# The recurrent branch's output projection as seven products of halves, with the pool branch's output tiles ahead

## The chip, the cores and the metric

The kernel runs on one core of a Trainium2 chip. The metric is the device time of one execution in microseconds. The core's engines work side by side, each through its own list of instructions in order: TensorE (PE in the profile, with its weight loads as PEld) multiplies matrices into eight PSUM banks, VectorE (DVE), ScalarE (ACT) and GpSimd (POOL) do the elementwise work, and SyncE (SP) issues DMA transfers. POOL issues some too. An instruction starts when its engine has reached it and its operands are ready.

## The reference

One block of a hybrid decoder, for 512 tokens of width 1024, in float32. In short:

```
h    = rms_norm(x, g_mix_pre)
u_pool, xb, gb, gates = split(h @ w_in)          # 512, 1024, 1024, 2 x 1024 wide
y_pool = pool_mixer(u_pool) @ w_pool_out         # 512 -> 1024
y_rnn  = rg_lru_branch(xb, gb) @ w_rg_out        # 1024 -> 1024
m    = sigmoid(gate_0) * y_pool + sigmoid(gate_1) * y_rnn
x    = x + rms_norm(m @ w_o, g_mix_post)
x    = x + rms_norm(gated ConvFFN(rms_norm(x)))  # w_up (1024 -> 2 x 3072), w_down
x    = x + rms_norm(gated input embedding p)     # out
```

The change concerns the third and fourth of these lines, `y_rnn` above all: a product of a 512×1024 matrix (tokens × channels) with the 1024×1024 weight `w_rg_out`. The kernel keeps activations with channels on the 128 partitions and tokens along the free dimension.

## The kernel before

**Products.** A float32 product is made of three TensorE products: each operand is split into a high part (rounded to the type fp32r) and a low part (the rest), and `mm3` multiplies high by high, high by low and low by high (lines 220 to 222 of the profile). A split is a copy on ScalarE (`hi`) and a subtraction on VectorE (`lo`, line 190). Weights come as 512 KB tiles (128×1024) by SP into `raw`, and are split into `hi` and `lo`; each of the three has six buffers. The function `weight` asks for a weight and has the next four of a fixed list (`order`) loaded and split too.

**Seven products.** A product of two matrices that are cut into 2×2 blocks can be made of seven products of half blocks, with sums and differences of blocks on either side (Strassen's form). The kernel has this for `w_o`, `w_up` and `w_down`: the sums of weight blocks (numbers 4 to 7; 1 to 3 are plain blocks) are made in DRAM by DMAs that add, issued by POOL at the start (`sum_in_dram`: first 16 for `w_o`, then 16 for `w_up`; those of `w_down` come later). The activations' sums ("forms") are made by VectorE and then split. The two output projections `w_pool_out` and `w_rg_out` are plain before.

**Early blocks.** Ten weight blocks (products 3, 7 and 4 of `w_o`, two each, and four of `w_up`) are loaded, split and written back to DRAM as `parts`, high and low, ahead of time (`split_early`), and later loaded as `hi` and `lo` straight away. Each is one load and two writes of 512 KB on SP's queue.

**Order.** TensorE's list is in the order of the code. The other engines' lists are set by a scheduler by priorities that follow the code's order; `urgent` raises those of evacuations. SP's list holds all loads and the `parts` writes, in one order, so that a write whose source isn't ready holds up the loads behind it. The names in the order below: `raw`, `hi`, `lo` are weight tiles, `ps` a PSUM bank, `m`, `t`, `C`, `A` are activation tiles, `parts` and the `sum` tiles lie in DRAM. A number behind a name tells buffers apart.

**The stages around the change.** The loop over `IN_ORDER` makes the gates' 16 tiles (`gate_step`), with the pooling and its maps between them; from its step `EARLY_AT` = 20 on it splits one early block a step. At gate tiles 5 and 8 the recurrent branch's output is split (`rnn_split`). Then a loop over the eight output tiles m: four `mm3` for `w_pool_out` (12 matmuls of 512 columns), eight for `w_rg_out` (24), then three VectorE operations (gate times each bank, and their sum into `mq`, lines 879 to 881), and one more early block in each turn (six in all). Behind it comes `w_o` by seven products in the order `SERIAL` = 1, 2, 5, 6, 3, 7, 4, whose forms are made by `o_form` out of `mq`.

Of the kernel before, what the change touches and what calls it, by code (L numbers as in the profile page):

```python
# [14 lines left out]
P = 128  # L15
# [67 lines left out]
def block_kernel(  # L83
# [161 lines left out]
    def rows2(w, kp, h):  # L245
# [22 lines left out]
    def up_block(p, f):  # L268

        j = (f % 10 - 1) * NJ + 2 * p  # L270
        h = f // 10 - 1
        return w_up[j : j + 2, :, h * S : (h + 1) * S].rearrange("j p c -> p j c")

    usum = {(p, f): dram.tile([P, 2, S], F32, name=f"up{p}sum{f}") for p in UP_SUMS for f in (5, 6, 7, 4)}

    def sums_of(name):

        if name == "up":
            for p in UP_SUMS:
                for f, start, more in ((5, 11, 12), (7, 12, 22), (6, 5, 22), (4, 6, 21)):  # L280
                    yield usum[p, f], usum[p, start] if start < 10 else up_block(p, start), {}
                    yield usum[p, f], up_block(p, more), {"accum_op": ALU.add}
# [122 lines left out]
    def prep(key):  # L405
        if key[0] == "up" and key not in parts:
            up_form(*key[1:])
            return
        if key in parts:
            hi, lo = parts_of(D)  # L410
            for i, v in enumerate((hi, lo)):
                nc.sync.dma_start(v.bitcast(F32), parts[key][i])
            if key[0] == "up":
                hi, lo = (v.rearrange("p (j c) -> p j c", j=2) for v in (hi, lo))
            ready[key] = (hi, lo)
            return
        ap = src[key]
        n = 1
        for d in ap.shape[1:]:
            n *= d  # L420
        raw = wpool.tile([P, n], F32, tag="raw", name=nm("raw"), bufs=6)
        dst = raw if len(ap.shape) == 2 else raw.rearrange("p (k c) -> p k c", k=ap.shape[1])
        if key == order[0]:
            nc.sync.dma_start(xraw[0], x_t[0])
            for a, b in FIRST:
                nc.sync.dma_start(raw[:, a:b], ap.rearrange("p k c -> p (k c)")[:, a:b])
        else:
            nc.sync.dma_start(dst, ap)
        hi, lo = parts_of(n)
        if key == order[0]:  # L430
            for a, b in FIRST:
                ACT.copy(hi[:, a:b], raw[:, a:b])
                sub(lo[:, a:b], raw[:, a:b], hi[:, a:b].bitcast(F32))
        else:
            ins = ACT.copy(hi, raw)  # L435
            if key[0] == "wpg" and key[2] == 1:
                behind(ins, last_copy[0].ins.name)
            with tc.high_priority(offset=2 * URGENT if key[0] == "wpg" and key[2] == 0 else 300 if key[0] == "in" and key[1] >= 12 else 0):
                ins = sub(lo, raw, hi.bitcast(F32))
                low_of[key] = ins.ins.name  # L440
            if key[0] == "wpg" and key[2] == 1:
                behind(ins, last_low[0])
        ready[key] = (hi, lo)

    def weight(key, ahead=AHEAD):
# [235 lines left out]
    yh = [None, None]  # L681
    yl = [None, None]

    def rnn_out(cs):
        for c in cs:
            act(rg_t[c], rg_t[c], AF.Gelu_apprx_tanh)
            V.tensor_tensor(r_t[c], r_t[c], rg_t[c], ALU.mult)
# [32 lines left out]
    rnn_out(range(8))  # L720


    yp, pools = {}, {}

    def pool_tile(g):
        w = WINDOWS[g]
# [21 lines left out]
    def pool_map(g):  # L748
        pw = weight("pool_w")
        ps = bank()  # L750
        mm3(ps, pick(pw, g * P, (g + 1) * P), pools[g], True, True)
        hi, lo = slot(F32R), slot(F32R)
# [7 lines left out]
    def gate_tile(m):  # L760
        ps = in_tile(16 + m)
        g = slot()
        with tc.high_priority(offset=300):
            scaled(ps, g)
        act(g, g, AF.Sigmoid)
        gate[m] = g
        if m in SPLIT_AT:
            rnn_split(SPLIT_AT.index(m))

    for n, step in enumerate(IN_ORDER):  # L770
        split_early(1 if n >= EARLY_AT else 0)
# [64 lines left out]

    def o_form(f):

        h11, h12, h21, h22 = (halves(mq[k], b) for b in range(2) for k in range(2))
# [20 lines left out]
        return v[:, 0], v[:, 1]  # L860


    mq = [quad("A", F32), quad("A", F32)]
    for m in range(KD):
        w = weight(("wpo", m))
        pa = bank()
        for k in range(4):
            mm3(pa, pick(w, k * P, (k + 1) * P), yp[k], k == 0, k == 3)
        w = weight(("wrg", m))
        if m == KD - 1:  # L870
            o_form(1)
# [10 lines left out]
        if m == KD - 1:  # L882
            o_form(2)
        if m == PLE_AT:
            pled = dram.tile([S, D], F32, name="pled")
            pq = []
            for k in range(2):
# [60 lines left out]

        return tuple(v[c][b] for v in (h2h, h2l))

    def products(o, w, i, form, start):
        for k in range(4):
            lhs = tuple(v[:, i, k * P : (k + 1) * P] for v in w)
            rhs = tuple(v[:, k, :] for v in form)
            mm3(o, lhs, rhs, start and k == 0, k == 3, near, skip_group_check=True)

    def up_plain(f, b):
        for i in range(2):
            d = gb if f % 10 == 1 else ub
# [21 lines left out]
                V.scalar_tensor_tensor(h2n[t, h], res[h], r, g_pre[h], ALU.mult, ALU.mult)  # L981


    oz, o11, o12, od5 = ([bank(), bank()] for _ in range(4))
# [420 lines left out]
```

## Time and profile before

| | us |
|---|---|
| median of three runs | 704.36 (704.07 to 704.71) |
| profiled execution, its own time | 703.83 |
| its span, first to last instruction | 702.1 |
| TensorE busy | 696.5 |
| VectorE busy | 574.1 |
| ScalarE busy | 440.9 |
| GpSimd busy | 82.9 |
| pool output and recurrent output tiles on TensorE | 202.6 to 264.8 |

The busy time of an engine is that of the whole span; a stage can be limited by something else than the mean shows. A row of the windows gives the busy time of each engine in a stretch of the span, with the number of instructions in parentheses. A row of the timeline gives the start, the duration, the engine, the source line, the operation, output and input, and in brackets the engine's idle time before it and what ended that. A row of the DMA view gives a queue's packets, its megabytes and the share of the 16 DMA engines' time that they took.

### The profile page before, as it was taken

The numbers are of one execution on the slowest core, as the hardware profiler recorded it, in microseconds if no ns is written. First come the engines' busy times: TensorE is split into PE (matmuls) and PEld (weight loads), VectorE is DVE, ScalarE is ACT, GpSimd is POOL, SyncE is SP. The second block draws the span as 40 slices with busy tenths as digits, with TensorE's granted clock in tenths as the row PEclk, the third lists the DMA queues.
The fourth block names the chain that finished last, engine by engine and source line by source line (L and its number), as shares of the span: only waits on it lengthen the run. The fifth ranks groups of instructions, "written<-read, shape, count | busy, mean of one in ns | idle before, by whom it ended". The sixth has DMA issues, their size and how long they took to land.

```text
span 702.1 us, 11239 instructions
## 1 busy us (share of the span) xinstructions
PE 696.5 (99%) x4279; PEld 637.0 (91%) x4279; DVE 574.1 (82%) x749; ACT 440.9 (63%) x670; POOL 82.9 (12%) x107
## 2 busy tenths in 40 slices
PE   9999999999999999999999999999999999999997
PEld 8888888888888888899999999999999888888886
DVE  5698645999656568777989999997999999788972
ACT  6857789953543245468866667765767766665631
POOL 0221111110000000121013232121300000001100
PEclk9999999999999999999999999999999999999999
DMA  8999986656698999996479999998976577868111
GB/s 320 406 314 244 227 229 153 157 165 219 237 327 285 323 334 374 332 317 218 152 286 240 278 297 266 304 239 299 241 200 233 203 250 235 283 206 273 47 61 60
DMA packets 65077, 172.54 MB, mean 246 GB/s; under 512 B 5952, under 2 KB 6592, under 8 KB 64704
## 3 DMA queue, kind: packets, MB, share of 16 engines
q1 hardware_dynamic: 50480, 129.88, 53.2%
q0 software_dynamic: 14400, 41.95, 25.5%
q8 instruction: 33, 0.54, 0.3%
q14 instruction: 20, 0.16, 0.1%
q10 hardware_dynamic: 144, 0.00, 0.0%
HBM read 155.03 MB, written 58.72 MB: 304 GB/s over the span
## 4 chain that ended last, share of the span: by engine, by line
PE 99%; DVE 0%; ACT 0%; issue 0%
PE ps L220 31%; PE ps L222 31%; PE ps L221 31%; PE ps L541 3%; PE ps L913 1%; PE ps L650 1%; PE ps L239 1%; PE ps L592 0%; ACT t L165 0%; DVE t L1323 0%; DVE t L1324 0%; PE ps L1034 0%; DVE m L231 0%; DVE mhalf L233 0%
## 5 line engine op out<-in xcount | busy, mean ns | idle before, releaser
L190 DVE TENSOR_TENSOR lo<-raw,hi 128x1024 fp32r<-128x1024 f32 (+2 forms) x193 | 224.0, 1184 | 60.2 <-ACT hi L435 42.3
L220 PE MATMUL ps<-A,hi 128*128 128x256 f32 (+1 forms) x608 | 194.4, 320 | 0.0
L221 PE MATMUL ps<-A,hi 128*128 128x256 f32 (+1 forms) x608 | 193.8, 319 | 0.0
L222 PE MATMUL ps<-A,lo 128*128 128x256 f32 (+1 forms) x608 | 193.8, 319 | 0.0
L435 ACT CAST hi<-raw 128x1024 fp32r<-128x1024 f32 (+1 forms) x112 | 112.0, 1011 | 80.6 <-PE ps L222 27.6
L220 PEld LDWEIGHTS ps<-A,hi 128*128 128x128 f32 x608 | 115.9, 191 | 8.2 <-issue 1.0
L222 PEld LDWEIGHTS ps<-A,lo 128*128 128x128 f32 x608 | 116.0, 191 | 6.8
L221 PEld LDWEIGHTS ps<-A,hi 128*128 128x128 f32 x608 | 116.0, 191 | 6.8
L220 PE MATMUL ps<-C,hi 128*128 128x256 f32 (+1 forms) x392 | 114.5, 292 | 0.0
L222 PE MATMUL ps<-C,lo 128*128 128x256 f32 (+1 forms) x392 | 114.3, 292 | 0.0
L221 PE MATMUL ps<-C,hi 128*128 128x256 f32 (+1 forms) x392 | 114.3, 292 | 0.0
L194 ACT CAST hi<-raw 128x1024 fp32r<-128x1024 f32 x78 | 80.3, 1050 | 24.5 <-PE ps L221 14.5
L220 PE MATMUL ps<-hi,A 128*128 128x512 f32 x224 | 85.2, 380 | 0.0
L221 PE MATMUL ps<-lo,A 128*128 128x512 f32 x224 | 84.9, 379 | 0.0
L222 PE MATMUL ps<-hi,A 128*128 128x512 f32 x224 | 84.9, 379 | 0.0
L220 PEld LDWEIGHTS ps<-C,hi 128*128 128x128 f32 x392 | 74.7, 191 | 1.9
L221 PEld LDWEIGHTS ps<-C,hi 128*128 128x128 f32 x392 | 74.7, 191 | 1.8
L222 PEld LDWEIGHTS ps<-C,lo 128*128 128x128 f32 x392 | 74.7, 191 | 1.7
L462 POOL TENSOR_TENSOR s<-s,mhalf 128x1 f32<-128x1 f32 (+1 forms) x21 | 16.2, 773 | 336.9 <-DVE s L478 315.1
L220 PEld LDWEIGHTS ps<-hi,A 128*128 128x128 f32 x224 | 42.3, 189 | 6.3 <-ACT hi L435 0.3
L222 PEld LDWEIGHTS ps<-hi,A 128*128 128x128 f32 x224 | 42.3, 189 | 6.0
L221 PEld LDWEIGHTS ps<-lo,A 128*128 128x128 f32 x224 | 42.3, 189 | 5.8
(191 smaller groups left out, 1024.0 us busy)
## 6 DMA issues: line engine op xcount, KB each, us to landing
raw<-in_w_up_dram SPq DMA_DIRECT2D x46, 512.0 KB, 7.7
wdsum<-in_w_down_dram POOLq DMA_DIRECT2D x36, 512.0 KB, 9.2
raw<-in_w_in_dram SPq DMA_DIRECT2D x32, 512.0 KB, 6.9
raw<-wdsum SPq DMA_DIRECT2D x24, 512.0 KB, 4.5
raw<-in_w_down_dram SPq DMA_DIRECT2D x18, 512.0 KB, 4.0
wosum<-in_w_o_dram POOLq DMA_DIRECT2D x12, 512.0 KB, 9.0
wdsum<-wdsum POOLq DMA_DIRECT2D x12, 512.0 KB, 6.9
parts<-hi SPq DMA_DIRECT2D x10, 512.0 KB, 5.0
```

The costliest lines, as they stand in the source:

```text
L190: return V.tensor_tensor(o, a, b, ALU.subtract)
L194: last_copy[0] = ACT.copy(hi, src)
L220: PE.matmul(o, ah, bh, start=start, stop=False, **kw)
L221: PE.matmul(o, ah, bl, start=False, stop=False, **kw)
L222: PE.matmul(o, al, bh, start=False, stop=stop, **kw)
L239: PE.matmul(wps[:, :P], ones, ones, start=True, stop=True)
L435: ins = ACT.copy(hi, raw)
L462: last_pow[0] = nc.gpsimd.tensor_tensor(y, v, mhalf[:, :n], ALU.pow).ins.name
L541: PE.matmul(rx[m], a[:, o : o + P], turns(b), start=k == 0 and i == 0, stop=k == KD - 1 and i == 2)
L650: PE.matmul(ps, bd[pr, a, o], turns(b[pr]), start=i == 0, stop=i == 2)
L913: PE.transpose(ps[:, q * P : (q + 1) * P], a[:, q * P : (q + 1) * P], ident)
```

## The change

The eight `w_pool_out` tiles are all made first, each into a bank of its own, and multiplied by the gate at once (line 918 of the changed kernel). Then `w_rg_out` is made by seven products in the order `RSEVEN` = 1, 5, 6, 2, 3, 7, 4, in two groups of four output tiles: 2 groups × 7 products × 2 tiles × 4 steps × 3 matmuls = 336 of 256 columns, where 192 of 512 stood. The recurrent output's forms are made in place: form 1 at gate tile 5, form 4 at 8, the differences at 9 to 11, and the forms 5, 6, 3 and 7 in the loop over the pool tiles, form 2 behind it. Partial sums of several products lie in shared banks, copied from one to another by ScalarE and merged with the gates by VectorE in `merge` (lines 931 to 934, 256 columns each, 20 operations a group). Eight sums of weight blocks are new, each made by two DMAs on POOL's queue, ahead of those of `w_o` and `w_up`. The early blocks start at step 16 in place of 20: eight are made in the gates' loop and two at the pool tiles 5 and 6. The copy of `p` into its form moves behind the first group.

```diff
-EARLY_AT = 20
-SPLIT_AT = 5, 8
+EARLY_AT = 16
+FORMS_AT, RSUMS_AT = {5: 1, 8: 4}, (9, 10, 11)
...
+RSEVEN = (1, 5, 6, 2, 3, 7, 4)
...
-PLE_AT = 3
+LATE_FORMS = {0: 5, 1: 6, 2: 3, 4: 7}
...
-        name: w.rearrange("(q a s p) c -> q s p a c", a=2, s=2, p=P) for name, w in (("wo", w_o), ("wd", w_down))
+        "wo": w_o.rearrange("(s q a p) c -> q s p a c", s=2, a=2, p=P),
+        "wd": w_down.rearrange("(q a s p) c -> q s p a c", a=2, s=2, p=P),
...
+    def rg_block(p, f):
+
+        j, h = 4 * p + 2 * (f % 10 - 1), f // 10 - 1
+        return w_rg_out[j : j + 2, :, h * S : (h + 1) * S].rearrange("j p c -> p j c")
+
+    rsum = {(p, f): dram.tile([P, 2, S], F32, name=f"rg{p}sum{f}") for p in range(2) for f in (5, 6, 7, 4)}
...
     for m in range(KD):
         plan(("wpo", m), w_pool_out[m])
-        plan(("wrg", m), w_rg_out[m])
+    for p in range(2):
+        for f in RSEVEN:
+            plan(("rg", p, f), rsum[p, f] if (p, f) in rsum else rg_block(p, {1: 11, 2: 21, 3: 22}[f]))
...
-    sum_in_dram(chain_of(sums_of("wo"), sums_of("up")), None)
+    sum_in_dram(chain_of(sums_of("rg"), sums_of("wo"), sums_of("up")), None)
...
-    def rnn_split(i):
-        yh[i], yl[i] = quad("C"), quad("C")
+    rform = {}
+
+    def rg_half(k, b):
+        return [r_t[4 * k + q][:, b * HALF : (b + 1) * HALF] for q in range(4)]
+
+    def rg_sum(o, a, b, op=ALU.subtract):
         for q in range(4):
-            split(yh[i][:, q, :], yl[i][:, q, :], r_t[4 * i + q])
+            V.tensor_tensor(o[q], a[q], b[q], op)
+
+    def rg_form(f):
+
+        h = [[rg_half(k, b) for b in range(2)] for k in range(2)]
+        if f == 3:
+            rg_sum(h[0][0], h[0][0], h[1][0], ALU.add)
+        v = {1: h[0][0], 2: h[1][0], 4: h[1][1], 5: h[1][1], 6: h[0][0], 3: h[0][0], 7: h[0][1]}[f]
+        w = quad("C" if f in (1, 2, 4) else "A").rearrange("p (s a) (b c) -> p s (a b) c", s=2, b=2)
+        for q in range(4):
+            split(w[:, 0, q, :], w[:, 1, q, :], v[q])
+        rform[f] = w[:, 0], w[:, 1]
...
-    mq = [quad("A", F32), quad("A", F32)]
+    mq, pas = [], []
     for m in range(KD):
         w = weight(("wpo", m))
-        pa = bank()
+        if m in LATE_FORMS:
+            rg_form(LATE_FORMS[m])
+        if m >= 5:
+            split_early(1)
+        pas.append(bank())
         for k in range(4):
-            mm3(pa, pick(w, k * P, (k + 1) * P), yp[k], k == 0, k == 3)
-        w = weight(("wrg", m))
-        if m == KD - 1:
-            o_form(1)
-        split_early(1)
-        pb = bank()
-        for k in range(KD):
-            y = yh[k // 4][:, k % 4, :], yl[k // 4][:, k % 4, :]
-            mm3(pb, pick(w, k * P, (k + 1) * P), y, k == 0, k == KD - 1)
-        a, b = gate[m], gate[8 + m]
+            mm3(pas[m], pick(w, k * P, (k + 1) * P), yp[k], k == 0, k == 3)
         with urgent():
-            V.tensor_tensor(row(a), back(pa), row(a), ALU.mult)
-            V.tensor_tensor(row(b), back(pb), row(b), ALU.mult)
-            V.tensor_tensor(mq[m % 2][:, m // 2, :], a, b, ALU.add)
+            V.tensor_tensor(row(gate[m]), back(pas[m]), row(gate[m]), ALU.mult)
+    rg_form(2)
+
+    rz, rd, rq = [bank(), bank()], bank(), {}
+    ra, rb2 = pas[4:6], pas[6:8]
+
+    def merge(p, n, i, b):
+
+        m, hs = 4 * p + 2 * n + i, slice(b * HALF, (b + 1) * HALF)
+        g, v = gate[8 + m][:, hs], (ra, rb2)[n][i][:, hs]
+        with urgent():
+            if n:
+                t = temp()[:, :HALF]
+                V.tensor_tensor(t, v, rq[p][:, i * HALF : (i + 1) * HALF], ALU.add)
+                v = t
+            V.tensor_tensor(row(g), back(v), row(g), ALU.mult)
+            V.tensor_tensor(mq[p][:, 2 * n + i, hs], gate[m][:, hs], g, ALU.add)
+
+    def rg_product(p, f):
+        for i in range(2):
+            w = weight(("rg", p, f))
+            o = {1: rz, 6: rz, 7: rz, 2: ra, 4: ra, 3: rb2, 5: (rd, rd)}[f][i]
+            a = HALF if f == 4 or (f, i) == (5, 1) else 0
+            products(o[:, a : a + HALF], w, i, rform[f], f in (1, 5), turns)
+            z = rz[i][:, :HALF]
+            with urgent():
+                if f == 1:
+                    ACT.copy(ra[i][:, :HALF], z)
+                elif (f, i) == (5, 1):
+                    rq[p] = temp()
+                    ACT.copy(rq[p], rd)
+                elif f == 6:
+                    ACT.activation(rb2[i][:, :HALF], z, AF.Identity, scale=-1.0)
+                elif f == 7:
+                    ACT.copy(ra[i][:, HALF:], z)
+                    ACT.activation(rb2[i][:, HALF:], z, AF.Identity, scale=-1.0)
+            if f in (2, 3, 7, 4):
+                merge(p, int(f in (3, 7)), i, int(f in (7, 4)))
+
+    for p in range(2):
+        for f in RSEVEN:
+            if f == 2:
+                mq.append(quad("C", F32))
+            rg_product(p, f)
+            if (p, f) == (1, 6):
+                o_form(1)
+            if (p, f) == (1, 3):
+                o_form(2)
+        if p == 0:
```

How the lists of three engines stand is shown at the places that the prediction speaks of. POOL's list, from the end of the first norm on, where the sums of weight blocks are issued; before:

```order
L295 DMA wosum_104<-in_w_o_dram 256x1x512 x4
L295 DMA wosum_106<-in_w_o_dram 256x1x512 x4
L295 DMA wosum_105<-wosum_104 16x8192 x2
L295 DMA wosum_105<-in_w_o_dram 256x1x512 x2
L295 DMA wosum_107<-wosum_105 16x8192 x2
L295 DMA wosum_107<-in_w_o_dram 256x1x512 x2
L295 DMA up1sum_112<-in_w_up_dram 256x1x512 x2
```

and changed:

```order
L304 DMA rg0sum_112<-in_w_rg_out_dram 256x1x512 x2
L304 DMA rg0sum_114<-in_w_rg_out_dram 256x1x512 x2
L304 DMA rg0sum_113<-rg0sum_112 16x8192
L304 DMA rg0sum_113<-in_w_rg_out_dram 256x1x512
L304 DMA rg0sum_115<-rg0sum_113 16x8192
L304 DMA rg0sum_115<-in_w_rg_out_dram 256x1x512
L304 DMA rg1sum_116<-in_w_rg_out_dram 256x1x512 x2
L304 DMA rg1sum_118<-in_w_rg_out_dram 256x1x512 x2
```

Sixteen DMAs for the recurrent weight stand first, and those of `w_o` and `w_up` follow in their old order.

SP's list at the end of the gates' loop, from the load of the last weight of that loop on; before:

```order
L428 DMA raw308_1728<-in_w_in_dram 128x1024
L355 DMA raw313_1762<-in_w_o_dram 128x2x512
L428 DMA raw316_1770<-in_w_pool_out_dram 128x512
L355 DMA raw321_1804<-in_w_o_dram 128x2x512
L889 DMA t391_2177<-in_p_t_dram 128x512
L889 DMA t394_2183<-in_p_t_dram 128x512
L428 DMA raw324_1812<-in_w_rg_out_dram 128x1024
L355 DMA raw329_1846<-wosum7_106 128x1024
L428 DMA raw332_1854<-in_w_pool_out_dram 128x512
L359 DMA parts3_120<-hi314_1764 128x1024
L359 DMA parts3_120<-lo315_1765 128x1024
```

and changed, from the row behind the same load on:

```order
L370 DMA parts3_128<-hi294_1704 128x1024
L370 DMA parts3_128<-lo295_1705 128x1024
L366 DMA raw317_1822<-wosum4_107 128x1024
L370 DMA parts4_129<-hi298_1718 128x1024
L370 DMA parts4_129<-lo299_1719 128x1024
L370 DMA parts5_130<-hi306_1764 128x1024
L370 DMA parts5_130<-lo307_1765 128x1024
L370 DMA parts6_131<-hi310_1778 128x1024
L370 DMA parts6_131<-lo311_1779 128x1024
L370 DMA parts7_132<-hi318_1824 128x1024
L370 DMA parts7_132<-lo319_1825 128x1024
L439 DMA raw320_1830<-in_w_pool_out_dram 128x512
```

The first pool-output weight stood ahead of all `parts` writes and stands behind ten of them now.

VectorE's list at the end of the stage, where `w_o`'s forms are made (`C467` and `C483` are the form of product 5, `A474` and the like its and other forms' low parts); before:

```order
L880 TENSOR_TENSOR m344_1927<-ps435_2392,m344_1927 128x512
L881 TENSOR_TENSOR A346_1931<-m275_1575,m344_1927 128x512
L190 TENSOR_TENSOR lo463_2485<-raw461_2482,hi462_2484 128x1024
L190 TENSOR_TENSOR A436_2420<-A346_1931,A436_2420 128x1024
L845 TENSOR_TENSOR C467_2513<-A345_1930,A346_1931 128x1024
```

and changed, the last rows up to the same form:

```order
L931 TENSOR_TENSOR t453_2689<-ps390_2192,t434_2538 128x256
L933 TENSOR_TENSOR m324_1861<-ps372_2116,m324_1861 128x256
L933 TENSOR_TENSOR m348_1987<-t453_2689,m348_1987 128x256
L934 TENSOR_TENSOR C439_2575<-m225_1343,m324_1861 128x256
L934 TENSOR_TENSOR C439_2575<-m274_1598,m348_1987 128x256
L933 TENSOR_TENSOR m332_1903<-ps379_2144,m332_1903 128x256
L191 TENSOR_TENSOR lo476_2760<-raw474_2757,hi475_2759 128x1024
L934 TENSOR_TENSOR C439_2575<-m240_1423,m332_1903 128x256
L191 TENSOR_TENSOR lo479_2785<-raw477_2782,hi478_2784 128x1024
L883 TENSOR_TENSOR C483_2813<-C405_2314,C439_2575 128x1024
```

Merges of 256 columns, up to three for one piece of an output tile, stand where two or three of 512 columns closed one tile.

More of the change, by code (lines that the diff above doesn't have):

```diff
@@ L272, in up_block @@
         return w_up[j : j + 2, :, h * S : (h + 1) * S].rearrange("j p c -> p j c")
+    def rg_block(p, f):
+        j, h = 4 * p + 2 * (f % 10 - 1), f // 10 - 1
+        return w_rg_out[j : j + 2, :, h * S : (h + 1) * S].rearrange("j p c -> p j c")
+    rsum = {(p, f): dram.tile([P, 2, S], F32, name=f"rg{p}sum{f}") for p in range(2) for f in (5, 6, 7, 4)}
     usum = {(p, f): dram.tile([P, 2, S], F32, name=f"up{p}sum{f}") for p in UP_SUMS for f in (5, 6, 7, 4)}
     def sums_of(name):
-        if name == "up":
-            for p in UP_SUMS:
+        if name in ("up", "rg"):
+            sums, of, ps = (usum, up_block, UP_SUMS) if name == "up" else (rsum, rg_block, range(2))
+            for p in ps:
                 for f, start, more in ((5, 11, 12), (7, 12, 22), (6, 5, 22), (4, 6, 21)):
-                    yield usum[p, f], usum[p, start] if start < 10 else up_block(p, start), {}
-                    yield usum[p, f], up_block(p, more), {"accum_op": ALU.add}
+                    yield sums[p, f], sums[p, start] if start < 10 else of(p, start), {}
+                    yield sums[p, f], of(p, more), {"accum_op": ALU.add}
             return
@@ L442, in prep @@
                 behind(ins, last_low[0])
+        if key[0] == "rg":
+            hi, lo = (v.rearrange("p (j c) -> p j c", j=2) for v in (hi, lo))
         ready[key] = (hi, lo)
@@ L837, in o_form @@
     def o_form(f):
-        h11, h12, h21, h22 = (halves(mq[k], b) for b in range(2) for k in range(2))
+        h11, h12, h21, h22 = (halves(mq[k], b) if k < len(mq) else None for b in range(2) for k in range(2))
         v = {1: h11, 2: h12, 4: h22}.get(f)
@@ L860, in o_lhs, with products @@
         return v[:, 0], v[:, 1]
[L863 removed]
+    def products(o, w, i, form, start, order=near):
+        for k in range(4):
+            lhs = tuple(v[:, i, k * P : (k + 1) * P] for v in w)
+            rhs = tuple(v[:, k, :] for v in form)
+            mm3(o, lhs, rhs, start and k == 0, k == 3, order, skip_group_check=True)
+    mq, pas = [], []
     for m in range(KD):
         w = weight(("wpo", m))
[L866 to L884 removed]
+        if m in LATE_FORMS:
[3 more added lines that the diff above has]
+        pas.append(bank())
+        for k in range(4):
+            mm3(pas[m], pick(w, k * P, (k + 1) * P), yp[k], k == 0, k == 3)
+        with urgent():
+            V.tensor_tensor(row(gate[m]), back(pas[m]), row(gate[m]), ALU.mult)
@@ L949, in h2 @@
         return tuple(v[c][b] for v in (h2h, h2l))
[L951 to L955, printed above, removed]
     def up_plain(f, b):
@@ L981, in x2_out @@
                 V.scalar_tensor_tensor(h2n[t, h], res[h], r, g_pre[h], ALU.mult, ALU.mult)
-    oz, o11, o12, od5 = ([bank(), bank()] for _ in range(4))
+    o11, o12 = ra, rb2
+    oz, od5 = ([bank(), bank()] for _ in range(2))
     o5 = wpool.tile([P, 2, S], F32, tag="sum", name=nm("sum"), bufs=1)
```

22 lines of the change are left out of this document (16 added, 6 removed).

## Prediction

> **What bounds the kernel now.** I read the engine shares and the chain first. The first row of the chain is TensorE alone, and no matmul group of the page has idle time before it: what is taken off TensorE shortens the run, and any wait put into TensorE lengthens it by its own length.
>
> ```profile
> span 702.1 us, 11239 instructions
> PE 696.5 (99%) x4279; PEld 637.0 (91%) x4279; DVE 574.1 (82%) x749; ACT 440.9 (63%) x670; POOL 82.9 (12%) x107
> PE 99%; DVE 0%; ACT 0%; issue 0%
> L221 PE MATMUL ps<-A,hi 128*128 128x256 f32 (+1 forms) x608 | 193.8, 319 | 0.0
> ```
>
> The second view is the table of windows, cut where the stages change: the gate tiles end at 202.6, the two output projections run to 264.8, then `w_o` begins. After each time range stand PE, PEld, DVE, ACT and POOL busy with their counts, the granted clock, the busy share of the 16 DMA engines, and GB/s.
>
> ```profile
> 162.00:182.00 20.00, 20.00 (x95) 17.44 (x94) 19.57 (x33) 10.71 (x16) 0.00 (x0) 1.00 0.49 172
> 182.00:202.60 20.60, 20.60 (x97) 18.05 (x96) 12.29 (x14) 8.99 (x12) 0.00 (x0) 1.00 0.94 338
> 202.60:264.80 62.20, 62.20 (x289) 54.45 (x289) 39.92 (x49) 23.59 (x29) 0.00 (x0) 1.00 0.90 313
> 264.80:301.00 36.20, 36.20 (x173) 31.73 (x172) 29.12 (x35) 18.04 (x30) 3.00 (x3) 1.00 0.96 350
> 400.00:500.00 100.00, 100.00 (x898) 100.00 (x897) 92.30 (x100) 63.84 (x106) 25.38 (x32) 1.00 0.99 279
> ```
>
> TensorE has no gap in any of them. But in the stage that changes, the DMA engines are 0.90 busy already and DVE has 22 us free. The third view shares each window between the two DMA queues: q1 carries SP's transfers, q0 the weight sums that POOL issues (packets, MB, share of the 16 engines). The rows are of 28–52 us (two queues at work), 202.6–264.8 and 264.8–301 (SP's alone).
>
> ```profile
> q1 hardware_dynamic: 1447, 5.27, 55.0%
> q0 software_dynamic: 1109, 2.96, 47.9%
> ```
> ```profile
> q1 hardware_dynamic: 7430, 19.40, 89.5%
> ```
> ```profile
> q1 hardware_dynamic: 4283, 12.64, 96.2%
> ```
>
> So SP's queue alone moved 12.64 MB in 36.2 us (349 GB/s), in the changed stage 312, and 219.6 GB/s while sums took half of the engines. "DMA: Bandwidth & Descriptors" of the Trainium skill, section "Queues, rings and completion order", says that each engine takes the queues with work in turn, a packet at a time; the 55.0% and 47.9% agree.
>
> **The change, TensorE's part.** The recurrent projection's 8×8×3 = 192 matmuls of 512 columns become 2×7×2×4×3 = 336 of 256. The stage 202.6–264.8 holds 288 wide ones: 62.2/288 = 0.216 us each. For narrow ones, at full clock:
>
> ```profile
> 419.73 0.28 PE L220 MATMUL ps<-C,hi 128*128 128x256 f32 x1
> ...
> 424.87 0.28 PE L221 MATMUL ps<-A,hi 128*128 128x256 f32 x1
> ```
>
> 46 steps in 5.14 us are 0.1117 each. 192×0.216 = 41.5; 336×0.1117 = 37.5: **−4.0 us**, all on the path. Moving the eight pool-output tiles forward changes no count. A smaller piece with a sign of its own: product 7 is followed at once by product 4, which accumulates on ScalarE's copy of 7; I price that at 0 (other bounds: 0 to 2×0.6).
>
> **VectorE's part.** Durations are pitches of back-to-back work: two 1024-wide ones take 2.25 us from 141.81 to 144.06 (1.125 each, 1.135 with the hand-over), six 512-wide ones 3.62 (0.60). A 256-wide one is 426 ns against 689 in the tail's rows; with the same overlap of 0.09 its pitch is 0.34.
>
> ```profile
> 141.81 2.34 DVE L190 TENSOR_TENSOR lo<-raw,hi 128x1024 fp32r<-128x1024 f32 x2
> 144.06 3.70 DVE L687 TENSOR_TENSOR m<-m,C 128x512 f32<-128x512 f32 x6
> 147.68 0.69 DVE L736 TENSOR_TENSOR t<-t 128x512 f32<-128x512 f32 x1
> L1323 DVE TENSOR_TENSOR t<-t,A x9: 426/689/693, 664.2 to 698.1; 128x512 f32<-128x512 f32 x7, 128x256 f32<-128x256 f32 x2
> ```
>
> The new forms' differences in gate tiles 9 to 11 (12×0.34 = 4.1 us) lie in 182–202.6, where DVE has 8 us free: 0. From the low part of group 0's last weight (product 4) to the form of `w_o`'s product 5, the changed order has 19 DVE instructions of 1024 columns, 2 of 512 and 40 of 256: 21.6+1.2+13.6 = 36.4 us. TensorE needs for the same stretch 8 products of 24×0.1117 and two of `w_o` of 24×0.216: 21.4+10.4 = 31.8. The form is late by **+4.6 us**. Ends: 0, if the scheduler's rows at the edge slip past the form, and +8, if each of the some 30 hand-overs in it costs 0.1 more.
>
> **SP's queue, which carries the sum.** SP issues in order, so a load behind a write that isn't ready waits with it. The rows of before:
>
> ```profile
> 159.92 0.38 SPq L355 DMA_DIRECT2D raw<-in_w_o_dram  x1
> 164.09 0.33 SPq L428 DMA_DIRECT2D raw<-in_w_pool_out_dram  x1
> 183.36 0.33 SPq L359 DMA_DIRECT2D parts<-hi  x1
> 184.68 0.33 SPq L359 DMA_DIRECT2D parts<-lo  x1
> ```
>
> There the first pool-output weight is issued at 164.09, used at 202.6. In the changed order five early blocks stand ahead of it with their ten `parts` writes, of which the first waits for its split. VectorE holds that split up to about where it had it before (the twelve differences go ahead), so I start at 183.4, the row of before. From there to the last weight of group 0 SP's queue carries 20 writes and 6 loads of early blocks (26×0.524 = 13.6 MB), 8 pool-output weights (2.1) and 7 of the recurrent branch (3.7): 19.4 MB. That weight's product starts at 202.6 + 96×0.216 + 6×24×0.1117 = 239.4 without a wait, and its cast and low part take some 2.2 us: it must have landed by 237.2. At 349 GB/s 19.4 MB take 55.6 us, to 239.0, 1.8 late; at 219.6 throughout they take 88 us, to 272, 35 late.
>
> Which? POOL's sums ended with the row at 156.07 before; 16 more come.
>
> ```profile
> 24.15 1.57 POOL L295 DMA_DIRECT2D wosum<-in_w_o_dram  x2
> 79.71 1.19 POOL L295 DMA_DIRECT2D up1sum<-in_w_up_dram  x1
> 156.07 1.03 POOL L295 DMA_DIRECT2D up2sum<-in_w_up_dram  x1 [3.56 <-DMA up2sum<-up2sum]
> 290.00 0.57 POOL L462 TENSOR_TENSOR s<-s,mhalf 128x1 f32<-128x1 f32 x1 [132.91 <-DVE s L478]
> ```
>
> The sixteen of `w_up` took 79.7 to 161, 5 us each; put off behind the 32 others they run 162 to about 243, that is through all of this stretch. But they don't keep q0 full: each waits for its predecessor's landing. I take 300 GB/s, just under the stage's own 312, the nearest row: 64.7 us, to 248.1, **+10.9 us**. Part of this is late at the pool-output tiles already, the rest at the recurrent products. Two smaller terms at 0: later writes of `parts` and the `p` loads lie behind this, and POOL's power of the first norm (290.00) has 45 us from the last sum; had each sum taken 8 us that would be gone.
>
> **Sum**, against the profiled run's own 703.83 (0.5 under the median of 704.36): 703.8 − 4.0 + 10.9 + 4.6 = 715.3, say 715.
>
> **Rivals.** *A, the waits don't come, and it is faster.* The window 400–500 speaks for it: this very pattern of seven products, sums on POOL, DMA at 0.99 and DVE at 92.30 of 100, and no gap in TensorE. It holds if SP's queue keeps some 350 GB/s, or its first `parts` writes go out 5 us earlier than I take, and DVE's forms slip ahead: −4.0, with the copies' 1 us and 1 of DVE: 702. Against it: in 400–500 q1 moved less, since 279 GB/s were both queues. *B, sums and SP's queue share the engines throughout*. The rows of 80–160, where most of the sums ran, speak for it: q0 held half of the engines with SP's queue at 22.5%.
>
> ```profile
> q0 software_dynamic: 3004, 8.62, 50.9%
> q1 hardware_dynamic: 1722, 6.01, 22.5%
> ```
>
> At 219.6 GB/s to 243 and 349 from there, 19.4 MB end at 183.4 + 59.6 + (19.4−13.1)/0.349 = 261, 24 late; VectorE's wait is partly covered then: 703.8−4+24+3 = 727. It decides if sums are at work in the whole of 183–243. Against it: the sums slow down too when SP's queue is full (10.5 us to land in 28–52 against 7.3 later), and each waits for the one before.
>
> ```profile
> wosum<-in_w_o_dram POOLq DMA_DIRECT2D x6, 512.0 KB, 10.5
> ```
> ```profile
> up2sum<-in_w_up_dram POOLq DMA_DIRECT2D x6, 512.0 KB, 7.3
> ```
>
> *C, the clock falls after the waits.* The first matmuls of the run are longer than the same shape later, at the granted clock of 1.00 of the windows above:
>
> ```profile
> L239 PE MATMUL ps<-m x18: 421/421/580, 1.1 to 4.8; 128*128 128x128 f32 x18
> L913 PE MATMUL ps<-ident,m x32: 272/273/273, 298.5 to 325.5; 128*128 128x128 f32 x32
> ```
>
> 18×(421−272) = 2.7 us is what a cold start costs. If each wait of several us costs that again, two of them add 5.4: 720.5. "TensorE: Matmul & The Clock Gate", Part 1, has the clock halved after an idle window of about 3.4 us, which would do this; before has no such wait, so its trace can't say. *D, product by product the waits cancel:* the −4.0 is spent on one short wait, 704.
>
> **How the numbers follow.** My forecast (waits of 6 to 24 us in all, 706 to 724) has 0.50, C 0.09, B 0.13, A 0.24, D 0.04. The range, 701.5 to 728, runs from A to B; it leaves out about 0.05 below, where the waits and copies vanish and DVE gains something, and 0.10 above, where the rate of B holds past 243 as well. Within the forecast case alone it is 706 to 724. About 0.2% (1.4 us) is what a measurement can tell from no change: faster by more 0.24 (A), within 0.04 (D), slower by more 0.72.
>
> **What would show it.** TensorE's narrow matmuls of the stage at 0.112 us apart with no gaps would show the −4.0. Waits of TensorE for pool-output or recurrent weights (`hi` or `lo` of a raw tile, behind a load) between 205 and 250, and SP's loads issued a few us ahead of use instead of 38, show the queue; a wait for `A` of `w_o`'s product 5 shows VectorE. Sums on POOL ending near 243, and q1 near 300 GB/s in 183–248, show the rate. I am wrong if the pool-output loads go out by 185 all the same, or if q1 stays at 350 with the sums beside it; then A holds. A first power on POOL pushed past 290 by sums still running would be a cost that I have at nothing.

## The result, and the profile after

The changed kernel takes 733.81 us (median of 4 runs, 732.32 to 735.04), the kernel before 704.22 beside it: a ratio of 1.0419, with a 95% interval of 1.0397 to 1.0442. That is 29.6 us slower, and outside the range I gave (701.5 to 728). The profiled execution's span grew from 702.1 to 731.4.

From the page of the changed kernel: TensorE's share falls from 99% to 96%, 7 us more of it are busy, and the chain now has DMA and VectorE in it.

```profile
span 731.4 us, 11678 instructions
PE 703.4 (96%) x4423; PEld 644.8 (88%) x4423; DVE 595.6 (81%) x815; ACT 458.2 (63%) x714; POOL 95.7 (13%) x123
PEclk9999999999987989999999999999999999999999
PE 82%; DMA 8%; DVE 5%; issue 2%; ACT 2%; SPq 1%; ACTq 0%; DVEq 0%
```

The windows of the changed stage (columns as before) place the loss: between 202.6 and 275 TensorE is busy 51 of 72 us, at granted clocks of 0.77, 0.86 and 0.86, while the DMA engines are at 0.93 to 1.05.

```profile
182.00:202.60 20.60, 20.60 (x98) 18.00 (x96) 10.21 (x12) 8.23 (x10) 2.28 (x3) 1.00 0.98 271
202.60:225.00 22.40, 12.51 (x38) 8.88 (x36) 9.01 (x16) 7.37 (x16) 3.30 (x4) 0.77 1.05 362
225.00:250.00 25.00, 21.45 (x108) 18.78 (x108) 19.14 (x31) 14.15 (x25) 2.58 (x3) 0.86 1.04 336
250.00:275.00 25.00, 17.47 (x129) 17.08 (x130) 17.69 (x31) 11.88 (x19) 0.00 (x0) 0.86 0.93 326
275.00:300.00 25.00, 24.67 (x192) 23.42 (x190) 23.75 (x40) 16.30 (x25) 0.00 (x0) 1.00 0.90 310
```

TensorE's waits in its timeline are five: three for casts of pool-output weights (tiles 0, 2 and 3), two at the tiles of group 0's product 6. (Two of 0.33 us follow, at 292.0 and 300.4.)

```profile
209.32 0.80 PE L221 MATMUL ps<-C,hi 128*128 128x512 f32 x1 [6.38 <-ACT hi L446]
218.77 0.48 PE L221 MATMUL ps<-C,hi 128*128 128x512 f32 x1 [2.07 <-ACT hi L446]
227.89 0.80 PE L221 MATMUL ps<-C,hi 128*128 128x512 f32 x1 [4.30 <-ACT hi L446]
251.51 0.38 PE L221 MATMUL ps<-A,hi 128*128 128x256 f32 x1 [2.17 <-ACT ps L945]
259.14 0.58 PE L221 MATMUL ps<-A,hi 128*128 128x256 f32 x1 [6.02 <-ACT ps L945]
```

By the distance from one matmul's start to the next, these five take 22.0 us above a normal step, and all the other steps from 150 to 320 together 11.1 us more than the normal 0.2157 and 0.1117 (0.35 before). Of these 11.1, 9.5 lie in stretches right behind four of the waits, in which the steps of 512 columns are 0.43 us: matmuls at the halved clock. The account closes: −4.0 + 22.0 + 11.1 = 29.1, and the span grew by 29.3.

Behind the waits stand late loads. On SP's timeline the first pool-output weight, issued at 164.09 before, goes out at 199.30, behind ten `parts` writes that began at 176.43; POOL's last sum is issued at 246.00, where the last stood at 156.07; and the queues' rows for 183 to 253 show what SP's queue got, 16.84 MB in 70 us (241 GB/s).

```profile
176.43 0.73 SPq L370 DMA_DIRECT2D parts<-hi  x1
...
199.30 0.58 SPq L439 DMA_DIRECT2D raw<-in_w_pool_out_dram  x1
```
```profile
246.00 1.03 POOL L304 DMA_DIRECT2D up2sum<-in_w_up_dram  x1 [5.20 <-DMA up2sum<-up2sum]
```
```profile
q1 hardware_dynamic: 6094, 16.84, 63.8%
q0 software_dynamic: 1912, 5.58, 37.7%
```

The last wait has one more link that the prediction didn't have. Product 6 adds into the bank that product 1 left, so ScalarE's copy of it (line 945) must be done first. On ScalarE's timeline the second tile's copy (258.72) stands behind the cast of a weight that is needed only three products later, and this cast waits for its load:

```profile
251.10 0.36 ACT L945 COPY ps<-ps 128x256 f32<-128x256 f32 x1
257.77 1.04 ACT L446 CAST hi<-raw 128x1024 fp32r<-128x1024 f32 x1 [6.31 <-DMA raw<-rg0sum]
258.72 0.37 ACT L945 COPY ps<-ps 128x256 f32<-128x256 f32 x1
```

### The profile page after: what moved, and what is told of

Same layout as the page of the kernel before. It is cut to its first block, busy times and chain, and to the rows that moved or that the text cites. A ratio compares the mean times of both kernels' runs of the same rounds, so it can differ in the third digit from the quotient of the medians.

```text
span 731.4 us, 11678 instructions
## 1 busy us (share of the span) xinstructions
PE 703.4 (96%) x4423; PEld 644.8 (88%) x4423; DVE 595.6 (81%) x815; ACT 458.2 (63%) x714; POOL 95.7 (13%) x123
## 4 chain that ended last, share of the span: by engine, by line
PE 82%; DMA 8%; DVE 5%; issue 2%; ACT 2%; SPq 1%; ACTq 0%; DVEq 0%
PE ps L221 26%; PE ps L222 26%; PE ps L223 25%; DMA raw<-in_w_up_dram 3%; PE ps L554 3%; DVE lo L191 2%; DMA parts<-hi 2%; DMA raw<-in_w_pool_out_dram 1%; DMA raw<-rg0sum 1%; PE ps L995 1%; PE ps L663 1%; ACT hi L195 1%; DMA raw<-in_w_rx_dram 1%; DVE t L770 1%; ACT hi L446 1%
## 5 line engine op out<-in xcount | busy, mean ns | idle before, releaser
L191 DVE TENSOR_TENSOR lo<-raw,hi 128x1024 fp32r<-128x1024 f32 (+2 forms) x199 | 230.9, 1184 | 68.7 <-ACT hi L446 43.6
L221 PE MATMUL ps<-A,hi 128*128 128x256 f32 (+1 forms) x672 | 213.0, 317 | 8.2 <-ACT ps L945 8.2
L223 PE MATMUL ps<-A,lo 128*128 128x256 f32 (+1 forms) x672 | 212.1, 316 | 0.0
L222 PE MATMUL ps<-A,hi 128*128 128x256 f32 (+1 forms) x672 | 212.1, 316 | 0.0
L446 ACT CAST hi<-raw 128x1024 fp32r<-128x1024 f32 (+1 forms) x118 | 118.8, 1013 | 72.8 <-PE ps L223 28.0
L221 PEld LDWEIGHTS ps<-A,hi 128*128 128x128 f32 x672 | 128.8, 192 | 16.7 <-ACT ps L945 8.6
L223 PEld LDWEIGHTS ps<-A,lo 128*128 128x128 f32 x672 | 128.9, 192 | 6.8
L222 PEld LDWEIGHTS ps<-A,hi 128*128 128x128 f32 x672 | 128.9, 192 | 6.7
L221 PE MATMUL ps<-C,hi 128*128 128x256 f32 (+1 forms) x408 | 119.4, 293 | 13.1 <-ACT hi L446 12.8
L222 PE MATMUL ps<-C,hi 128*128 128x256 f32 (+1 forms) x408 | 118.5, 291 | 0.0
L221 PEld LDWEIGHTS ps<-C,hi 128*128 128x128 f32 x408 | 80.1, 196 | 16.3 <-ACT hi L446 14.3
L223 PEld LDWEIGHTS ps<-C,lo 128*128 128x128 f32 x408 | 79.8, 196 | 2.2 <-DVE lo L191 0.9
L222 PEld LDWEIGHTS ps<-C,hi 128*128 128x128 f32 x408 | 79.9, 196 | 1.4
L304 POOL DMA_DIRECT2D wdsum<-in_w_down_dram x36 | 33.4, 1092 | 110.1 <-ACT ps L1118 53.4
```

What stands on the lines that cost most here:

```text
L191: return V.tensor_tensor(o, a, b, ALU.subtract)
L221: PE.matmul(o, ah, bh, start=start, stop=False, **kw)
L222: PE.matmul(o, ah, bl, start=False, stop=False, **kw)
L223: PE.matmul(o, al, bh, start=False, stop=stop, **kw)
L304: ins = nc.gpsimd.dma_start(o, i, **kw)
```

## The experiments

The first four ask which part of the 29.6 us belongs to the clock, to the sums' traffic, to the order on SP's queue and to the order of the sums.

**Work in place of the waits.** Extra matmuls ahead of the five waits keep TensorE busy; they write banks that are overwritten or unused.

```diff
+        filler(pas[m], {0: 30, 2: 20, 3: 30}.get(m, 0))
         for k in range(4):
             mm3(pas[m], pick(w, k * P, (k + 1) * P), yp[k], k == 0, k == 3)
...
+            if (p, f) == (0, 6):
+                filler(bank(), (24, 29)[i])
             products(o[:, a : a + HALF], w, i, rform[f], f in (1, 5), turns)
```

> The changed kernel with extra matmuls, whose results are overwritten or unused, put in front of the five waits that TensorE has in the changed kernel's stage (30, 20 and 30 of 512 columns ahead of pool-output tiles 0, 2 and 3, 24 and 29 ahead of the two tiles of group 0's product 6), about as long as the waits with the clock at full. It tells how much of the 11.1 us that matmuls at the halved clock took longer is a cost of its own. If the clock's fall is a cost on top of the waits: 733.8 - 11.1 = 723. If each wait ends when its load has landed, so that a faster clock only waits longer for the next load, only the slow matmuls behind the last wait (259.1 to 264.5, half of 5.4 us) are won: 733.8 - 2.7 = 731. In both, the granted clock has no 0.5 in 200 to 270.

Measured: 732.55 us, and in its windows TensorE is busy all the time at a clock of 1.00.

```profile
202.60:225.00 22.40, 22.40 (x102) 18.90 (x101) 10.33 (x17) 8.93 (x17) 3.31 (x4) 1.00 1.07 360
225.00:250.00 25.00, 25.00 (x139) 22.20 (x138) 17.01 (x29) 11.73 (x21) 2.58 (x3) 1.00 1.03 362
250.00:275.00 25.00, 25.00 (x179) 23.13 (x178) 19.48 (x34) 13.34 (x23) 0.00 (x0) 1.00 0.81 285
```

By the medians 1.3 us are won, which lies within the spread of the changed kernel's own runs (732.32 to 735.04). But that is not the price of the halved clock, because the fillers outlast the waits. In front of the last of the five tiles the filler (line 909 of this run) fills TensorE until the tile's first matmul at 260.90, while ScalarE's copy (line 952 here, 945 in the changed kernel), the last thing that this tile needs (its weight's low part is ready at 242.7), is done at 255.15:

```profile
254.31 6.76 PE L909 MATMUL ps<-C 128*128 128x512 f32 x29
254.79 0.36 ACT L952 COPY ps<-ps 128x256 f32<-128x256 f32 x1
260.90 0.27 PE L221 MATMUL ps<-A,hi 128*128 128x256 f32 x1
```

The changed kernel begins the same tile at 259.14, 1.8 us earlier, although its loads are later (product 7's weight is cast at 257.77 there, at 253.83 here). Had the filler ended with the copy, up to 5.7 us more could have been won, an estimate from these rows. So the halved clock costs between nothing and some 7 us, and this run doesn't say how much; that it came near the second of the expected times owes as much to the fillers' length as to the reason given there.

**Without the new sums.** The products 4 to 7 of the recurrent branch load plain blocks of the same size (another output).

```diff
-            plan(("rg", p, f), rsum[p, f] if (p, f) in rsum else rg_block(p, {1: 11, 2: 21, 3: 22}[f]))
+            plan(("rg", p, f), rg_block(p, {1: 11, 2: 21, 3: 22, 5: 12, 6: 21, 7: 22, 4: 11}[f]))
...
-    sum_in_dram(chain_of(sums_of("rg"), sums_of("wo"), sums_of("up")), None)
+    sum_in_dram(chain_of(sums_of("wo"), sums_of("up")), None)
```

> The changed kernel without the sixteen new sums on POOL's queue: the products 4 to 7 of the recurrent branch load a plain block of the weight instead, of the same size (the output is another one). SP's queue, VectorE, ScalarE and TensorE have the same work. If the two queues' sharing of the DMA engines is what makes SP's loads late (q1 242 GB/s in 183 to 253), the sums end near 162, q1 gets some 340, and TensorE's waits of 22 us shrink to under 6: 702 to 710. If SP's queue is late because its writes and loads wait for splits and for each other in order, with the rate of little account: 722 to 732.

Measured: 710.01 us, 23.8 less than the changed kernel. With q0 empty, SP's queue moves 24.05 MB in the same 70 us (344 GB/s):

```profile
q1 hardware_dynamic: 9890, 24.05, 95.0%
```

The sums' share of the DMA engines is the main cause. What remains, 6 us above before with TensorE still waiting 6.8 us in the stage, comes with this queue full at 95%.

**The early blocks later.**

```diff
-EARLY_AT = 16
+EARLY_AT = 20
...
             rg_product(p, f)
+            if (p, f) in ((0, 3), (0, 7), (0, 4), (1, 1)):
+                split_early(1)
```

> The changed kernel with the early blocks split later: four in the gates' loop (from step 20 as before), two at pool tiles 5 and 6, four in the recurrent products (behind products 3, 7, 4 of group 0 and 1 of group 1). The traffic is the same, but fewer parts writes stand ahead of the pool-output loads. If the order on SP's queue is the cause, the three waits at the pool tiles (13.5 us with the clock's loss behind them) go, and part of those at product 6: 712 to 720. If the rate is the cause, the waits only move to the recurrent products and the early blocks' reloads: 727 to 735.

Measured: 735.87. The waits moved (to 208, 217, 243, 264 and on) and nearly kept their sum: 20.2 us by the brackets of its timeline up to 320, where the changed kernel has 21.6. The place of the writes in SP's list is not what counts, as long as the bytes must pass in the stretch.

**The sums of two groups in turn.** For `w_rg_out` and for `w_up`: both groups' starts, then both adds, so that POOL needn't wait out each landing.

```diff
-            for p in ps:
-                for f, start, more in ((5, 11, 12), (7, 12, 22), (6, 5, 22), (4, 6, 21)):
-                    yield sums[p, f], sums[p, start] if start < 10 else of(p, start), {}
-                    yield sums[p, f], of(p, more), {"accum_op": ALU.add}
+            for f, start, more in ((5, 11, 12), (7, 12, 22), (6, 5, 22), (4, 6, 21)):
+                for p in ps:
+                    yield sums[p, f], sums[p, start] if start < 10 else of(p, start), {}
+                for p in ps:
+                    yield sums[p, f], of(p, more), {"accum_op": ALU.add}
```

> The changed kernel with the sums of the recurrent weight and of w_up issued for both groups in turn (start of group 0, start of group 1, then the adds), as those of w_o are, instead of one group after the other. Each sum waits for its own start; in the changed kernel the chained ones took 4.9 us (recurrent) and 6.4 us (w_up) each, those of w_o 3.1. At 3.3 to 3.6 us each 48 end at 185 to 200 instead of 255. If the sharing of the DMA engines is the cause: 706 to 718. If order on SP's queue is: 725 to 733. If sums in a denser row hurt the in-projection's loads ahead of 183: slower than 734.

Measured: 716.13, a gain of 17.7 us by the order of issue alone. The last sum is issued at 184.89 in place of 246.00, so that in the stage SP's queue has the DMA engines to itself:

```profile
184.89 1.04 POOL L305 DMA_DIRECT2D up2sum<-in_w_up_dram  x1 [1.24 <-DMA up2sum<-up2sum]
```

TensorE still waits 10.3 us there, between 198 and 285.

**Sums in the kernel before.** The other side of the second run: before, with the sixteen sums put ahead on POOL's queue and not used.

```diff
-    sum_in_dram(chain_of(sums_of("wo"), sums_of("up")), None)
+    sum_in_dram(chain_of(sums_of("rg"), sums_of("wo"), sums_of("up")), None)
```

> The kernel before, with the changed kernel's sixteen new sums on POOL's queue ahead of the others, their results unused. TensorE, VectorE and SP's order as before; only q0 works until about 250 in place of 162. If the sharing of the DMA engines alone costs the time, SP's queue falls from 312 to some 245 GB/s in 203 to 250 and before's head start of 38 us for its loads is used up in part: 706 to 720. If the new order of the changed kernel is needed for a loss, and before's head start covers it: 703 to 705.

Measured: 724.25, 20.6 us over before, with not one TensorE instruction changed. In 202.6 to 250 SP's queue gets 10.54 MB where it had 14.67 (222 GB/s for 310), the first row this run's, the second that of before:

```profile
q1 hardware_dynamic: 3437, 10.54, 62.1%
```
```profile
q1 hardware_dynamic: 5545, 14.67, 89.5%
```

So before had its loads ahead of use, but not by enough. Two opposite edits, +20.6 and −23.8, say the same of the sums.

**Without the sums, and with early blocks later.** Both edits of the second and third run.

> Two edits at once: no new sums on POOL (plain blocks loaded in their place, another output), and the early blocks split later as in the run on that. Without the new sums alone the time is 710.0, with TensorE waiting 6.8 us in five places and DMA engines at 95% in 183 to 253. If those waits are due to the order on SP's queue (parts writes ahead of loads), they go now: 702 to 705. If they are due to the bytes that SP's queue has to move in the stretch, they stay or move behind: 708 to 714.

Measured: 718.74 in two runs that differ (716.63 and 720.84), above the 710.01 of the one edit. TensorE waits in ten places from 228 to 338, 10.8 us in all, 2.6 of them behind 300. So putting the early blocks later doesn't win back what the 710 still lose; it costs more.

**Fewer bytes.** Sums in turn, and only the six early blocks of `w_o`; `w_up`'s four are loaded raw and split at their use.

```diff
-    early = [("wo", f, q) for f in SERIAL[4:] for q in range(pieces["wo"])] + [("up", 0, f) for f in PLAIN]
+    early = [("wo", f, q) for f in SERIAL[4:] for q in range(pieces["wo"])]
...
-EARLY_AT = 16
+EARLY_AT = 18
```

> The changed kernel with the sums issued for both groups in turn (716.1 alone), and with six early blocks in place of ten: the four of w_up are loaded raw and split where they are used, from step 18 of the gates' loop on. Each early block is one load, two writes and two loads of 512 KB where a plain one is one load: 4 x 1.57 MB less in 183 to 253 and as much reloading later. If the bytes that the DMA engines have to move there are what remains, 6.3 MB at 340 GB/s are 18 us of their time, and the waits (10.5 us) go: 701 to 706. If VectorE misses its early work behind 265, where it is busy 29 of 36 us: 705 to 712.

Measured: 712.39. TensorE's waits in the stage shrink from 10.3 to 4.6 us, and a new one of 3.9 appears near 320.

**Fewer bytes and fewer sums.** The same, with the sums of `w_up`'s pair 2 left to VectorE.

```diff
-UP_SUMS = (1, 2)
+UP_SUMS = (1,)
```

> As the run with sums in turn and six early blocks, and the sums of w_up's pair 2 not made in DRAM but by VectorE, as those of the later pairs are: eight sums less on POOL, five additions of 1024 columns (5.7 us) more on VectorE near 340, where it has 2 to 4 us free in 20, and one load more. If the queues' sharing still costs, it goes: 699 to 704. If VectorE's five additions make a wait there: 703 to 710.

Measured: 707.38 (706.53 to 708.23). One wait of 0.3 us is left in the stage: its matmuls run from 203.5 to 262.6, 59.1 us where before took 62.2, at a clock of 1.00, and VectorE is busy 57.74 of 62.2:

```profile
202.60:264.80 62.20, 61.88 (x448) 58.54 (x447) 57.74 (x103) 40.43 (x70) 0.00 (x0) 1.00 0.91 309
```

The wait near 320 is still there. Its table of TensorE's waits (us in total, times, longest) has it on top:

```profile
PE ps L221 <- ACT m L833: 3.9, 1, 3.9
PE ps L240 <- DVE mhalf L234: 1.1, 1, 1.1
```

ScalarE empties the embedding's banks (line 833) behind squares of a norm, for which VectorE is late (3.22 us of idle time on ScalarE, ended by VectorE's line 985):

```profile
318.58 0.63 ACT L481 ACTIVATE rb<-m 128x512 f32<-128x512 f32 x1 [3.22 <-DVE m L985]
```

**The same edits on the kernel before.** Six early blocks and `UP_SUMS = (1,)` there.

> The kernel before with two of those edits: six early blocks and no DRAM sums for pair 2 of w_up. It has no waits that they could take away: 703.5 to 704.5. If VectorE is short of time behind 265 or near 340: 705 to 708.

Measured: 710.90, with the same single wait near 320:

```profile
PE ps L220 <- ACT m L794: 3.9, 1, 3.9
```

So these two edits cost 6.9 us by themselves (704.01 without them, beside it). With them in both, the changed kernel (707.38) is 3.5 us faster than the one before, or 3.0 by the ratios to the kernel before that ran beside each (1.0052 and 1.0095): most of the shorter matmuls' 4.0. Two differences stay: the early blocks start at step 18 in the one and at 20 in the other, and the changed kernel still has its sixteen sums; issuing them in turn has no counterpart in the kernel before, where a single group is left.

**All ten early blocks kept.** As the run with fewer bytes and fewer sums, but with ten early blocks, and with the norms behind the embedding tiles (the edit of the next run).

> The same edits with all ten early blocks kept: the four of w_up are split in the stage again, 6.3 MB more for SP's queue in 183 to 265 and 4.5 us less for VectorE behind it. If the bytes in the stage bind, TensorE waits there again: 706 to 712. If eight sums less are enough: 700 to 703.

Measured: 711.47, with waits of 1.6, 0.6, 1.0 and 2.4 us between 211 and 238. The last sum is issued at 166.54, ahead of the stage; SP's queue fills 95.4% of the engines' time in 183 to 253, so its own bytes bind with the sums out of the way.

**Two attempts to take the last wait away.** First, the norms behind the four embedding tiles:

```diff
             x2_sum(3, (oz[1], o5[:, 1]))
-            x2_out(3)
-            ple_norm(0, outs0)
-        if t == 0:
-            outs0 = outs
-        else:
-            ple_norm(t, outs)
+        pouts.append(outs)
+    x2_out(3)
+    for t in range(NT):
+        ple_norm(t, pouts[t])
```

> As the run with sums in turn, six early blocks and pair 2's sums by VectorE (707.4, no wait of TensorE left in 200 to 270, one of 4.2 us at 318 for a PSUM bank that ScalarE empties behind four squares of a norm that wait for VectorE), with one edit more: the last token tile's second norm and the embedding's norms are placed behind all four embedding tiles in the code, so that ScalarE empties those banks first. If that order on ScalarE was the wait, it and the slow matmuls behind it (1.7 us) go: 701 to 702.5. If VectorE is late by itself, the transposes of the last tile (some 326) wait instead: 705 to 708.

Measured: 707.38 (ratio 1.0042, 1.0028 to 1.0056). The wait at 318 is gone, and one for the last tile's split, 10 us later, takes its place:

```profile
PE ps L221 <- ACT C L195: 2.5, 1, 2.5
```

Then the embedding's norms behind that split as well; in the code their loop moves from behind the embedding tiles to behind the plain products that follow:

```diff
-        s = rstd_of(outs, in_order=False)
+        s = rstd_of(outs, in_order=False, after=h2_done[0])
...
-    for t in range(NT):
-        ple_norm(t, pouts[t])
...
         up_plain(f, 1)
+
+    for t in range(NT):
+        ple_norm(t, pouts[t])
```

> As the run with the last norms placed behind the embedding tiles (707.4), and the embedding's four norms made to follow the last token tile's split on ScalarE. In that run TensorE waited 2.8 and 1.1 us at 327 to 331 for that split, which stood behind six squares of these norms (326.2 to 329.2 us), and ran 3.4 us at the halved clock. If these are what is left of the loss, they go, and the time is 707.4 - 3.9 - 1.7 = 701.8, below the kernel before by 2 us, what is left of the 4.0 of the shorter matmuls. If the norms now come in the way later, between the up products' own evacuations: 704 to 707.

Measured: 707.50 (1.0045, 1.0027 to 1.0063). The wait moves on again, to 347, and one of 1.8 us stands at the stage's end. The profile is that of the longest of the four executions (709.24; the others took 707.22 to 707.54), so the 1.8 may belong to it alone:

```profile
PE ps L221 <- ACT ps L1124: 4.0, 1, 4.0
PE ps L221 <- ACT ps L953: 1.8, 1, 1.8
```

I did not find a version that beats before. The last wait only moved: 3.9 us, then 2.5 and 0.8, then 4.0. That VectorE's work in 265 to 350 is the reason is argued from ScalarE's idle row above, and wasn't isolated.

## Why the prediction was wrong

- **The shorter matmuls, −4.0: right.** With the same side edits in both kernels the gain is 3.0 to 3.5 us, and the stage takes 59.1 us against 62.2. The copy of product 7's bank, which I had at nothing, is the wait of 0.33 us at 292.0.
- **SP's queue, +10.9: the right mechanism, three times too small.** This is the step that failed: TensorE came to product 4 of group 0 at 271.15, where the prediction has 239.4 without a wait, so it was 31.7 us late. Two things in the term were wrong.
- **First, the rate: 12.2 of the missing 20.8 us.** I took 300 GB/s, "just under the stage's own 312, the nearest row". The queue got 241. The nearest row was that of 28 to 52 us, 219.6 GB/s, since that is where both queues work; the stage's own row belonged to a stretch without sums. The first write went out a little before 183.4 (at 176.43), but the last weight of group 0 could be cast only at 260.25, where I had it landed at 248.1 (19.4 MB at 241 GB/s take 80 us). Its low part ended at 262.5: 23.1 us late, for 10.9.
- **Second, the place of the wait: 8.6 us.** I let TensorE run up to the product whose weight is late. It stood at the second tile of product 6 until 259.14, for ScalarE's copy out of a bank behind the cast of product 7's weight, and still had three and a half products to do when that wait ended. So product 4 began 8.6 us behind its own weight; 2.6 of these are matmuls at the halved clock behind that wait. What is queued behind a waiting cast on its engine was not in my account. These 8.6 us are read from the timeline; no run takes this one wait away by itself.

```profile
260.25 1.04 ACT L446 CAST hi<-raw 128x1024 fp32r<-128x1024 f32 x1 [1.16 <-DMA raw<-rg0sum]
261.32 1.23 DVE L191 TENSOR_TENSOR lo<-raw,hi 128x1024 fp32r<-128x1024 f32 x1 [1.25 <-ACT hi L446]
271.15 0.28 PE L221 MATMUL ps<-C,hi 128*128 128x256 f32 x1
```

- **The reason I gave for 300 was wrong.** I wrote that the sums "don't keep q0 full: each waits for its predecessor's landing". They do wait, but where both queues press they only take longer, and last longer: the sixteen of `w_up` took 152.8 to about 255, 6.4 us each for 5 predicted, and q0 still had 37.7% of the engines in 183 to 253.
- **VectorE's +4.6: the work was there, the wait wasn't.** The instructions from the low part of product 4's weight to the split form of `w_o`'s product 5 took 261.3 to 302.2. But I let that stretch begin just in time, and its first result stood ready at 262.5, 8.6 us before TensorE came to it: TensorE had waited at product 6 already. A wait that comes first pays for those behind it; the two terms don't add.
- **Rival B** (the queues share throughout, 727, chance 0.13) is what happened. It has the last weight landed at 261 and 24 us late, against the cast at 260.25 and 23.1. That is in part luck: its rate until 243 was too low (219.6 for 241), and it let the sums end at 243 and not at about 255. What it lacks is the 8.6 us of the wait's place; the 3 us for VectorE that it added didn't come.
- **Rival C** (the clock falls; its sum is 720.7, not 720.5): the clock fell, and the granted clock was 0.77 in the window with the 6.38 us wait. "TensorE: Matmul & The Clock Gate" of the Trainium skill, Part 1, has it halve after an idle window of about 3.4 us. The trace agrees in part: slow matmuls follow the waits of 6.38, 4.30 and 6.02 us, but also that of 2.07 us, which is shorter (from 220.03 on the steps are 0.37 to 0.43 us in place of 0.216), and none follow that of 2.17. What it cost is open, between nothing and some 7 us, for 5.4 predicted.
- **Rival A** (the load keeps ahead, 702) rested on the window 400 to 500, where sums and the same product pattern go together without a gap. I noted against it that both queues together moved 279 GB/s there. That note was the better reading: SP's queue moved only 10.79 MB in those 100 us (108 GB/s).

## What to carry to other kernels

Before adding transfers on a second queue, take the first queue's rate from a window in which both are at work, and count the bytes that it must move until the last deadline; the stage here, at a DMA share of 0.90 and without a wait, had no room for sixteen more transfers (20.6 us). Follow also what stands behind a waiting instruction on its engine: a late load can stop TensorE at a product that doesn't use it. Sums in DRAM that depend on each other are best issued in turn over independent groups, so that they end early: here the order of issue alone was worth 17.7 us. A gain on the bound engine is paid out only as far as the engines next to it keep their lead; measure it against the old kernel under the same side edits.

## What the runs showed that I had not expected

- Filler matmuls that outlast a wait hide what they are to measure: TensorE was busy throughout at a clock of 1.00, and came to the last of the five tiles 1.8 us later than with the waits.
- A chained sum (a copy and an add, each waiting for the last) took 4.9 us in 24 to 103, and one of `w_o`'s, whose pieces take turns, 3.1 in 103 to 152, at the same 512 KB. With the recurrent ones issued in turn too, they took 3.5 each, in 24 to 79.
- The kernel before, at 99% TensorE, loses 20.6 us to sixteen transfers that no engine waits for.
